# One projection of a hybrid trunk by one Strassen level, with sums that stay in PSUM and another place in the program

## The chip, the cores and the metric

The kernel runs on one core of one Trainium2 chip. The metric is the device time of one execution in microseconds (us). It is a float32 kernel whose large products run on TensorE (PE); VectorE (DVE), ScalarE (ACT), GpSimd (POOL) and the DMA queues of SyncE (SP) and POOL prepare operands and move data.

## The reference

One layer with D = 1024, 1024 tokens, batch 1, all in float32. What matters here:

```
h = RMSNorm_pre(x)
[s5_x | s5_gate | lru_x | lru_gate | merge_gate_s | merge_gate_l] = h @ W_in
S5 : y = Re(C s) + D u (diagonal SSM), GELU, GLU with w_glu (512 -> 2x512),
     times SiLU(s5_gate), then ps = y @ w_bs       (512 -> 1024)
LRU: conv, RG-LRU over 10 heads of 128 channels, times SiLU(lru_gate),
     then pl = yl @ w_bl                           (1280 -> 1024)
merged = sigmoid(merge_gate_s) * ps + sigmoid(merge_gate_l) * pl
mix = merged @ W_out                               (1024 -> 1024)
x = x + RMSNorm_post(mix); x = x + (p @ W_ple) * sigmoid(x @ W_ple_gate)
```

The change concerns `yl @ w_bl`: 8 output rows of 128 channels, each a sum over 10 heads, for 1024 tokens.

## The kernel before

**A product.** Every fp32 operand is split in two float32r parts, high and low. A 128x128 weight block times 512 tokens is then three matmuls (`three`: high x high, high x low, low x high) of 128x512, all into one PSUM bank of 128x512. A row of 8 weight blocks for all 1024 tokens is 48 matmuls; a w_bl row with its 10 heads is 60.

**Weights.** `W` streams them. A chunk of 512 KB (`wraw`, four buffers) comes over SP's queue; per group of four blocks ("quad"; `wq`, a ring of six) ACT copies the high part and DVE subtracts for the low part (L228, "a low"). For w_bs, w_out's plain part and w_ple_gate the low part is instead an ACT copy with a minus sign and an accumulating DMA from POOL's queue (L220). `W.ahead` prepares up to four quads ahead of the one in use, and `fetch` loads raw chunks further ahead; a quad in a plain product feeds 24 matmuls. Where one Strassen level is used (parts of W_in, and w_out), POOL adds up the weight sums (L188), and a quad then feeds 12 matmuls.

**Order.** PE, DVE, ACT and POOL issue in the order in which the program is written; the order on SP's queue is the scheduler's. Work that is written as a generator in `bg` (splits, merges) is advanced one step at each `tick`, between quads. PSUM has eight 128x512 banks: two belong to other products, and from the RG-LRU stage until after F the other six are three tiles of two banks (`wide`), which the products take in turn.

**The stages around the change.** `light(6)`, `light(7)` are two rows of W_in (silu gates of S5; `ps_L`, evicted by ACT L950 and DVE L952). Meanwhile head 9 of the RG-LRU ends on DVE with a scan over 1024 tokens (L1031) and a product (L1034). Then `bl((0, 1))`, `bl((2,))`: w_bl rows 0, 1, 2; the GLU products `eb0, ea0 ... eb3, ea3` (4 blocks each); w_bl rows 3 to 7; F: the eight rows of w_bs, each multiplied with its gate `gs` (`mg`, L1234), to which an accumulating DMA on POOL's queue (L1235) adds the row that `bl` left in DRAM (`ms_d`). The generator `merged` (L1176 to L1223) turns the finished `mg` rows into the operands of the Strassen w_out products, `mB`, `mT`. w_out begins with `oX` (operand `mB11` for four products, then `mB21` accumulated onto them), and goes on with `oY`, `oZ`, `oW`, `oV`.

The operands of w_bl, `yl` (high and low for each head), fill 10 pages of SBUF; head 9's raw row goes to DRAM (`yl_d`) and comes back. What is written of `bl` is short:

```
def bl(ds):
    for d in ds: load blg{d} from sgl_d
    products of 10 heads into ps (two rows share a pass where len(ds) > 1)
    V.tensor_tensor(gs[d], gs[d], t, ALU.mult)       # L1108, 128x1024
    nc.sync.dma_start(ms_d[d], gs[d])                # L1109
```

## Time and profile before

| | us |
|---|---|
| median of 3 runs (range) | 962.07 (961.91 to 962.28) |
| the profiled execution, its own time | 961.16 |
| span of its profile | 959.4 |
| PE busy | 945.0 of 959.4 (98%), 4308 matmuls |
| DVE, ACT, POOL busy | 598.8, 452.7, 161.0 |
| DMA moved | 128.19 MB |
| w_bl rows 0 to 2 | 582.0 to 622.8 |
| GLU | 622.8 to 667.15 |
| w_bl rows 3 to 7 | 667.15 to 735.0 |
| F | 735.0 to 780.8 |
| first oX products of w_out | 780.8 to 799.6 |

The profiled execution is 0.91 us below the median; 1.76 us of its time lie outside the span. Times in rows are microseconds from the start of the span. A line number is that of the kernel, or of the helper that issues the instruction: all matmuls of `three` carry L309, L310, L311. A matmul's duration (0.39 us for 128x512) overlaps the next one; the pitch from start to start is what it costs.

Of the kernel before, what the change touches and what calls it, by code (L numbers as in the profile page):

```python
# [36 lines left out]
def weight_plan():  # L37
# [11 lines left out]
    def col(name, m, ks):  # L49
        return [(name, k, m) for k in ks]  # L50
# [196 lines left out]
def tile_hybrid_trunk(  # L247
# [29 lines left out]
    yl_d = dram.tile([P, NT], F32, name="yl_d")  # L277
# [701 lines left out]
    yl_home = {m: i for m, i in enumerate((2, 3, 6, 7, 8, 9, 4, 5, 10, 11))}  # L979
    yl, yl_raw = {}, {}  # L980

    def yl_page(m):
        t = page(yl_home[m], f"yl{m}", F32).rearrange("p (s n) -> p s n", s=2)
        yl[m] = t.bitcast(F32R)
        return t

    def lru_head(m):
# [33 lines left out]
        def late():  # L1021
# [11 lines left out]
            t = l1.tile([P, NT], F32, tag=f"yr{m}", name=f"yr{m}") if m in (6, 7) else g  # L1033
            V.tensor_tensor(t, sq, g, ALU.mult)  # L1034
            yl_raw[m] = t
            if m == NL - 1:
                nc.sync.dma_start(yl_d, t)
            if m < 6:
                yl_page(m)
                S.activation(yl[m][:, 0], t, AF.Copy)  # L1040
                yield
                V.tensor_tensor(yl[m][:, 1], t, yl[m][:, 0].bitcast(F32), ALU.subtract)
# [51 lines left out]
    def ylr(k, h):  # L1094
        return yl[k][:, 0, HALF[h]], yl[k][:, 1, HALF[h]]

    def bl(ds):
        gs = {}
        for d in ds:
            gs[d] = h2.tile([P, NT], F32, tag=f"g{d % 2}", name=f"blg{d}")  # L1100
            nc.sync.dma_start(gs[d], sgl_d[d])
        if len(ds) > 1:
            ps = [wide(f"ps_bl{d}") for d in ds]
            two(NL, ylr, "bl", ps=[[t[:, HALF[h]] for h in range(2)] for t in ps])
        else:
            ps = [rows(ylr, f"bl{ds[0]}", nk=NL)]
        for t, d in zip(ps, ds):
            V.tensor_tensor(gs[d], gs[d], t, ALU.mult)  # L1108
            nc.sync.dma_start(ms_d[d], gs[d])  # L1109

    bg.append(gel_build())
    bl((0, 1))
    bl((2,))
    drain()

    ysf = [page(i, f"ysf{i}", F32).rearrange("p (k n) -> p k n", k=2) for i in range(2)]
# [6 lines left out]
    et = page(11, "et", F32).rearrange("p (i n) -> p i n", i=2)  # L1123
# [4 lines left out]
    def by_slot(t):  # L1128
        return t.rearrange("p (k j) -> p j k", j=8)

    ys = []
    for j in range(NS):
        t, y = et[:, j % 2], ysr(j)
        pb = rows(ger, f"eb{j}", nk=NS)
        S.activation(by_slot(t), pb.rearrange("p (j k) -> p j k", j=8), AF.Sigmoid)
        V.tensor_tensor(t, t, y, ALU.mult)
        pa = rows(ger, f"ea{j}", nk=NS)
        V.tensor_tensor(by_slot(y), by_slot(t), pa.rearrange("p (j k) -> p j k", j=8), ALU.mult)
# [12 lines left out]
    for d in range(3, ND):
        bl((d,))
    drain()

    mpg = ((7, 8, 12, 13), (14, 15, 16, 17))
# [15 lines left out]
    def op(name, i):  # L1171
        mop[name] = [quarter(page(i + s, f"m{name}{s}")) for s in range(2)]
# [310 lines left out]
```

### The profile page before, as it was taken

The page shows a single profiled execution, that of the slowest core. Times are in us where ns is not written, and L with a number is a line of the kernel's source. Part 1 is how long each engine was busy: PE and PEld are TensorE (multiplying, and loading weights), DVE is VectorE, ACT ScalarE, POOL GpSimd, SP SyncE. Part 2 cuts the span into 40 slices and gives each one's busy share as a digit, 9 for nine tenths or more (in the row PEclk, how much of TensorE's full clock was granted, in tenths as well). Part 3 has the DMA queues.
Part 4 walks back from the last instruction along what each step waited for, and adds up shares of the span by engine and source line. Part 5 has one row for each costly group of instructions (what it writes and reads, how often), then busy time and mean ns, then how long its engine had stood idle before and what let it go on. Part 6 is the DMA issues. An engine that isn't in the chain of part 4 may idle for free.

```text
span 959.4 us, 11815 instructions
## 1 busy us (share of the span) xinstructions
PE 945.0 (98%) x4308; PEld 775.4 (81%) x4308; DVE 598.8 (62%) x1019; ACT 452.7 (47%) x652; POOL 161.0 (17%) x178
## 2 busy tenths in 40 slices
PE   8999999999999999999999999999999999999998
PEld 6888888788888888888888888888888877887877
DVE  6976578788763337766666668245311469786842
ACT  6652243344343256676666665224112344558561
POOL 1318121222210000000000000000001244534431
PEclk9999999999999999999999999999999999999999
DMA  9754133323333201111111115742347995399995
GB/s 347 256 129 125 51 117 116 116 73 116 117 116 99 71 28 50 50 50 45 50 50 50 50 50 150 262 153 63 109 148 219 236 224 174 116 244 231 283 256 156
DMA packets 64282, 128.19 MB, mean 134 GB/s; under 512 B 18400, under 2 KB 29024, under 8 KB 64224
## 3 DMA queue, kind: packets, MB, share of 16 engines
q1 hardware_dynamic: 55584, 109.61, 35.2%
q0 software_dynamic: 8640, 17.83, 10.5%
q8 instruction: 34, 0.56, 0.2%
q14 instruction: 24, 0.20, 0.1%
HBM read 84.81 MB, written 27.79 MB: 117 GB/s over the span
## 4 chain that ended last, share of the span: by engine, by line
PE 77%; DVE 10%; issue 7%; DMA 2%; ACT 2%; POOL 1%; SPq 1%; POOLq 0%; DVEq 0%; ACTq 0%
PE ps_L L309 6%; PE ps_L L311 5%; PE ps_L L310 5%; PE ps_rx L309 4%; PE ps_rg L309 4%; PE ps_rg L311 4%; PE ps_rx L311 4%; PE ps_rg L310 4%; PE ps_rx L310 4%; PE ps_bl L310 4%; PE ps_bl L309 4%; PE ps_bl L311 4%; PE ps_pg L310 2%; PE ps_pg L311 2%; PE ps_pg L309 2%
## 5 line engine op out<-in xcount | busy, mean ns | idle before, releaser
L216 ACT ACTIVATE wq<-wraw 128x512 fp32r<-128x512 f32 (+1 forms) x189 | 112.3, 606 | 90.3 <-PE ps_bl L311 77.6
L220 POOL DMA_DIRECT2D wq<-wraw x52 | 47.8, 920 | 533.3 <-ACT wq L219 516.9
L309 PE MATMUL ps_L<-hB,wq 128*128 128x512 f32 x320 | 127.1, 397 | 0.0
L311 PE MATMUL ps_L<-hB,wq 128*128 128x512 f32 x320 | 124.7, 390 | 0.0
L310 PE MATMUL ps_L<-hB,wq 128*128 128x512 f32 x320 | 124.7, 390 | 0.0
L228 DVE TENSOR_TENSOR wq<-wraw,wq 128x512 fp32r<-128x512 f32 (+1 forms) x137 | 97.1, 728 | 4.7 <-ACT wq L216 4.7
L309 PEld LDWEIGHTS ps_L<-hB,wq 128*128 128x128 f32 x320 | 60.1, 188 | 13.4 <-issue 1.7
L311 PEld LDWEIGHTS ps_L<-hB,wq 128*128 128x128 f32 x320 | 60.1, 188 | 12.9
L310 PEld LDWEIGHTS ps_L<-hB,wq 128*128 128x128 f32 x320 | 60.1, 188 | 11.7
L997 DVE SCALAR_TENSOR_TENSOR c<-ps_rx,cp_t,c 128x1023 f32<-128x1023 f32 (+2 forms) x30 | 38.4, 1282 | 43.6 <-ACT c L995 42.9
L309 PE MATMUL ps_rx<-hB,wq 128*128 128x512 f32 x160 | 62.5, 391 | 0.0
L309 PE MATMUL ps_rg<-hB,wq 128*128 128x512 f32 x160 | 62.5, 391 | 0.0
L311 PE MATMUL ps_rx<-hB,wq 128*128 128x512 f32 x160 | 62.4, 390 | 0.0
L311 PE MATMUL ps_rg<-hB,wq 128*128 128x512 f32 x160 | 62.4, 390 | 0.0
L309 PE MATMUL ps_bl<-yl,wq 128*128 128x512 f32 x160 | 62.3, 389 | 0.0
L311 PE MATMUL ps_bl<-yl,wq 128*128 128x512 f32 x160 | 62.3, 389 | 0.0
L310 PE MATMUL ps_rx<-hB,wq 128*128 128x512 f32 x160 | 62.2, 389 | 0.0
L310 PE MATMUL ps_rg<-hB,wq 128*128 128x512 f32 x160 | 62.2, 389 | 0.0
L310 PE MATMUL ps_bl<-yl,wq 128*128 128x512 f32 x160 | 62.2, 389 | 0.0
L1108 DVE TENSOR_TENSOR blg<-blg,ps_bl 128x1024 f32<-128x1024 f32 x8 | 9.8, 1221 | 68.8 <-PE ps_bl L311 68.7
L950 ACT ACTIVATE sg<-ps_L 128x1024 f32<-128x1024 f32 x20 | 20.5, 1026 | 61.6 <-PE ps_L L311 45.1
L310 PE MATMUL ps_pg<-x1hl,wq 128*128 128x512 f32 x120 | 47.4, 395 | 0.8 <-DVE x1hl L1185 0.8
(347 smaller groups left out, 2184.7 us busy)
## 6 DMA issues: line engine op xcount, KB each, us to landing
wraw<-w_blocks SPq DMA_DIRECT2D x90, 512.0 KB, 4.1
wq<-wraw POOLq DMA_DIRECT2D x52, 256.0 KB, 6.6
xt<-x_t SPq DMA_DIRECT2D x8, 512.0 KB, 8.2
ple_d<-ple_sb SPq DMA_DIRECT2D x8, 512.0 KB, 4.9
sgl_d<-sg SPq DMA_DIRECT2D x8, 512.0 KB, 4.8
sgs_d<-sg SPq DMA_DIRECT2D x8, 512.0 KB, 4.6
blg<-sgl_d SPq DMA_DIRECT2D x8, 512.0 KB, 4.7
ms_d<-blg SPq DMA_DIRECT2D x8, 512.0 KB, 3.0
```

The lines of the kernel that those rows point to most:

```text
L216: nc.scalar.activation(hi, src, AF.Copy)
L220: nc.gpsimd.dma_start(lo.bitcast(F32), src, accum_op=ALU.add)
L228: self.nc.vector.tensor_tensor(lo, src, hi.bitcast(F32), ALU.subtract)
L309: T.matmul(ps, wh, xh, start=start, stop=False, skip_group_check=more)
L310: T.matmul(ps, wh, xl, start=False, stop=False, skip_group_check=more)
L311: T.matmul(ps, wl, xh, start=False, stop=stop, skip_group_check=more)
L950: S.activation(t, ps, AF.Sigmoid)
L997: V.scalar_tensor_tensor(c[:, d:], ps[:, :NT - d], w_[3 - d], c[:, d:], ALU.mult, ALU.add)
L1108: V.tensor_tensor(gs[d], gs[d], t, ALU.mult)
```

## The change

`w_bl` for heads 0 to 7 becomes a 2x2 Strassen product (Winograd's form, seven products): heads 0-3 and 4-7 against the two halves of the tokens, and pairs of output rows (2p, 2p+1). Heads 8 and 9 stay plain ("tails", `btail`). Per pair of rows the seven products are of four blocks for 512 tokens, 12 matmuls each.

- Ahead of GLU: products B11 for the four pairs (banks `bX0` to `bX3`), B21 accumulated onto the same banks, then the tails of the rows 0, 2, 4, 6 for the first half of the tokens, and their gates (`brow`, L1129). ACT keeps a copy of the B11 products (`bu`).
- GLU after it, each row in two banks evicted apart (`brows`).
- Then, for each of the four pairs: T2 into bank `bZ`, T1 into `bW`, a tail into `bV`, T3 onto `bZ`, a tail onto `bW`, B22 onto `bW`, a tail onto `bZ`, T4 onto `bZ`: 78 matmuls. The sums between products are made by DVE and ACT inside the banks.
- The operands (T1 to T4, B11, B21, B22: differences of token halves and heads, then the split) are new work on DVE and ACT: B21 after `light(7)`, T2 and T1 during GLU, T3, B22 and T4 between GLU and the first pair, and the split of the GLU's result `ys`, which stood in the GLU loop, during the first pairs.
- POOL makes the weight sums of the four pairs, 16 operations of 128x512.
- One pool of six single banks (`pp`) is opened after `light(7)` instead of after F, and F's rows are evicted by halves. `yl_d` and its round trip go.

Line numbers shift: L309 to L311 become L312 to L314, L228 becomes L232, L188 L192, L220 L224, L952 L958, L1034 L1054.

```diff
+    for ks in (lo, hi):                                   # order of the weights
+        for m in (0, 4):
+            plain(col("w_bl", m, ks) + col("w_bl", m + 2, ks))
+    plain([b for m in range(0, ND, 2) for b in col("w_bl", m, hi2)])
...
+        for part in ("O2", "S1", "P", "S3", "S4", "A22"):
...
+    lctx.close()
+    wide_ctx.close()
+    pp = ctx.enter_context(tc.tile_pool(name="pp", bufs=6, space=PSUM))
...
+    xs = [bank(f"bX{p}") for p in range(4)]
+    for p_ in range(4):
+        bprod(xs[p_], "B11", True)
+        S.activation(bu[:, p_, :], xs[p_], AF.Copy)
...
+    for p_ in range(4):
+        bprod(xs[p_], "B21", False)
...
+    def late_ops():
+        for name, i, j, q in (("T3", 12, 13, 12), ("B22", 14, 15, 22), ("T4", 0, 1, 21)):
+            bop(name, i, j)
+            for k in range(4):
+                bsplit(name, k, bq(q, k))
+            yield
+        yield
+        for j in range(NS):                                # split of ys
...
+    next(late_bl)
+    bg.append(late_bl)
+    for p_ in range(4):
...
+        z, w_, v = (bank(f"b{n}{p_}") for n in "ZWV")
+        bprod(z, "T2", True)
+        V.tensor_tensor(z, z, u, ALU.add)
+        S.activation(u, z, AF.Copy)
+        bprod(w_, "T1", True)
+        S.activation(gb[:, HT:], w_, AF.Copy)
+        V.tensor_tensor(w_, w_, u, ALU.add)
...
+        btail(v, wb[2:], 1, True)
...
+            three(z, b, (hi[:, k, :], lo[:, k, :]), False, k == 3, True)   # T3
...
+        btail(w_, wb[:2], 1, False)
...
+            three(w_, b, (hi[:, k, :], lo[:, k, :]), False, k == 3, True)  # B22
...
+        btail(z, wb[2:], 0, False)
+        bprod(z, "T4", False)
...
     for n, d in enumerate(F_ROWS):
         sgs_load()
-        ps = rows(ysr_, f"F{d}", nk=NS)
-        V.tensor_tensor(mgrow(d), gls[n], ps, ALU.mult)
+        for h, ps in enumerate(brows(ysr_, f"F{d}", NS)):
+            V.tensor_tensor(mgrow(d)[:, HALF[h]], gls[n][:, HALF[h]], ps, ALU.mult)
         G.dma_start(mgrow(d), ms_d[d], accum_op=ALU.add)
         bg.append(merged(d))
-    wide_ctx.close()
-    pp = ctx.enter_context(tc.tile_pool(name="pp", bufs=6, space=PSUM))
```

**Place 1, PE between `light(7)` and w_bl.** Before, the last matmuls of `light(7)` and the first of w_bl row 0 (`ps_bl0`, operand `yl0` and weights `wq102`):

```order
2445 L309 MATMUL ps_L7_4499<-hB220_440,wq101_4417 128x512
2446 L310 MATMUL ps_L7_4499<-hB221_441,wq101_4417 128x512
2447 L311 MATMUL ps_L7_4499<-hB220_440,wq101_4417 128x512
2448 L309 MATMUL ps_bl0_4630<-yl0_3076,wq102_4454 128x512 [waits PE_49,Activation_49]
2449 L310 MATMUL ps_bl0_4630<-yl0_3076,wq102_4454 128x512
2450 L311 MATMUL ps_bl0_4630<-yl0_3076,wq102_4454 128x512 [waits DVE_49]
2451 L309 MATMUL ps_bl0_4630<-yl0_3076,wq102_4454 128x512
```

Now, the same place, with the first product B11 (`bX0`):

```order
2445 L312 MATMUL ps_L7_4501<-hB220_439,wq101_4421 128x512
2446 L313 MATMUL ps_L7_4501<-hB221_440,wq101_4421 128x512
2447 L314 MATMUL ps_L7_4501<-hB220_439,wq101_4421 128x512
2448 L312 MATMUL bX0_4637<-bB112_2779,wq102_4458 128x512 [waits DVE_49]
2449 L313 MATMUL bX0_4637<-bB113_2780,wq102_4458 128x512
2450 L314 MATMUL bX0_4637<-bB112_2779,wq102_4458 128x512
```

The first matmul into `bX0` waits for DVE. The new pool gives `bX0` the bank that held the first half of `ps_L7`, whose last reader is DVE's L958; `ps_bl0` had another tile's banks. On DVE that reader stands at the end of head 9, as it did before (the scan and the two products ahead of it are the same, L1030, L1031, L1034, L952 there):

```order
726 L1050 TENSOR_TENSOR i9_4256<-i9_4256,ta9_4257 128x1024 [waits Activation_49]
727 L1051 SCALAR_TENSOR_TENSOR sq9_4258<-r9_4255,i9_4256 128x1024 [waits DVE_49]
728 L1054 TENSOR_TENSOR yr9_4569<-sq9_4258,g9_4254 128x1024 [waits DVE_49]
729 L958 TENSOR_TENSOR sg_7_4571<-sg_7_4571,ps_L7_4501 128x1024 [waits Activation_49]
730 L308 TENSOR_TENSOR bB211_4610<-yr2_3750,bB210_4609 128x512 [waits Activation_49] x2
731 L308 TENSOR_TENSOR bB211_4610<-yr3_4083,bB210_4609 128x512 [waits Activation_49] x2
```

What moved behind it: the splits of B21 and of heads 8 and 9 follow where the splits of heads 6 to 9 stood.

**Place 2, DVE from the end of GLU.** Before: the last GLU product, its split, head 9's row, the lows of the next quads, and the gate of w_bl row 3:

```order
763 L1138 TENSOR_TENSOR ysf1_4868<-et_4873,ps_ea3_5092 128x8x128 [waits DVE_49,PE_49]
764 L1141 TENSOR_TENSOR ys3_5125<-ysf1_4868,ys3_5125 128x1024 [waits Activation_49]
765 L228 TENSOR_TENSOR wq121_5093<-wraw69_4878,wq121_5093 128x512 [waits DMAHW4_49]
766 L1147 CAST yl9_5146<-yl9_5146 128x1024 [waits DMAHW3_49]
767 L1148 TENSOR_TENSOR yl9_5146<-yl9_5146 128x1024 [waits DVE_49]
768 L228 TENSOR_TENSOR wq122_5131<-wraw69_4878,wq122_5131 128x512 [waits Activation_49]
769 L228 TENSOR_TENSOR wq123_5162<-wraw70_5096,wq123_5162 128x256 [waits DMAHW2_49,Activation_49]
770 L1108 TENSOR_TENSOR blg3_5128<-blg3_5128,ps_bl3_5130 128x1024 [waits DMAHW6_49,PE_49]
```

Now, from the second half of the last GLU product to the add into `bW0` (x2 stands for two instructions; L308 is the low part of a split):

```order
785 L1207 TENSOR_TENSOR ysf1_4834<-et_4839,ps_ea31_5099 128x4x128 [waits PE_49]
786 L308 TENSOR_TENSOR bT313_5134<-yr0_3076,bT312_5133 128x512 [waits Activation_49] x2
787 L308 TENSOR_TENSOR bT313_5134<-yr1_3413,bT312_5133 128x512 [waits Activation_49] x2
788 L232 TENSOR_TENSOR wq123_5100<-wraw68_4848,wq123_5100 128x512 [waits DMAHW4_49,Pool_49]
789 L308 TENSOR_TENSOR bB2215_5166<-yr2_3750,bB2214_5165 128x512 [waits Activation_49] x2
790 L308 TENSOR_TENSOR bB2215_5166<-yr3_4083,bB2214_5165 128x512 [waits Activation_49] x2
791 L1237 TENSOR_TENSOR bZ0_5147<-bZ0_5147,bu_4636 128x512 [waits PE_49]
792 L232 TENSOR_TENSOR wq124_5150<-wS2_120_4962,wq124_5150 128x512 [waits Pool_49]
793 L232 TENSOR_TENSOR wq125_5177<-wraw68_4848,wq125_5177 128x512 [waits Activation_49]
794 L308 TENSOR_TENSOR bT41_5198<-yr2_3750,bT40_5197 128x512 [waits Activation_49] x2
795 L308 TENSOR_TENSOR bT41_5198<-yr3_4083,bT40_5197 128x512 [waits Activation_49] x2
796 L1241 TENSOR_TENSOR bW0_5148<-bW0_5148,bu_4636 128x512 [waits Activation_49]
```

Twelve splits of T3, B22 and T4 and three lows of quads now stand in one row around the two adds into banks, for which PE's products T3 (into `bZ0`) and the tail of `bW0` wait.

**Place 3, SP's queue before F.** Before, `gs0` and the first `gsp` are the gates of F's first two rows, `wraw80` is the last chunk of w_bs, `wraw81` and `wraw82` are the first two of w_out, `blg6`, `blg7` are w_bl's last rows:

```order
219 L1109 DMA ms_d_82<-blg5_5288 128x1024
220 L157 DMA wraw80_5403<-w_blocks 128x1024
221 L1101 DMA blg7_5448<-sgl_d_79 128x1024
222 L157 DMA wraw81_5455<-w_blocks 128x1024
223 L1109 DMA ms_d_82<-blg6_5370 128x1024
224 L1204 DMA gs0_5543<-sgs_d_80 128x1024
225 L157 DMA wraw82_5513<-w_blocks 128x1024
226 L1204 DMA gsp_5542<-sgs_d_80 128x1024
227 L1109 DMA ms_d_82<-blg7_5448 128x1024
228 L1204 DMA gsp_5542<-sgs_d_80 128x1024
229 L1204 DMA gs2_5546<-sgs_d_80 128x1024
230 L1204 DMA gs4_5580<-sgs_d_80 128x1024
```

Now (chunks count two higher: `wraw82` is the last of w_bs, `wraw83` the first of w_out; `ga2` to `gb3` are w_bl's last two pairs of rows, stored in halves; the first `gsp` is F's first gate):

```order
225 L1234 DMA gb3_5568<-sgl_d_79 128x512
226 L1130 DMA ms_d_82<-ga2_5437 128x512
227 L1233 DMA ga3_5567<-sgl_d_79 128x1024
228 L161 DMA wraw82_5615<-w_blocks 128x1024
229 L1130 DMA ms_d_82<-ga3_5567 128x512
230 L161 DMA wraw83_5650<-w_blocks 128x1024
231 L1130 DMA ms_d_82<-gb3_5568 128x512
232 L1315 DMA gsp_5709<-sgs_d_80 128x1024
233 L161 DMA wraw84_5680<-w_blocks 128x1024
234 L1130 DMA ms_d_82<-ga3_5567 128x512
235 L1315 DMA gsp_5709<-sgs_d_80 128x1024
236 L1315 DMA gs3_5714<-sgs_d_80 128x1024
```

Against the chunks the gates stand where they stood; between the last chunk of w_bs and F's first gate stood one load, one chunk and one store, and now a chunk and two half stores. What moved is the place of all of this against PE: a quad of the Strassen pairs feeds 12 matmuls where one of a plain row fed 24, so the four quads by which `W.ahead` and the chunks behind it run ahead of PE reach half as far before F's first product.

More of the change, by code (lines that the diff above doesn't have):

```diff
@@ L1092, in gel_build @@
             yield
[L1094 to L1109, printed above, removed]
@@ L1111, in tile_hybrid_trunk, with bprod, btail @@
-    bg.append(gel_build())
-    bl((0, 1))
-    bl((2,))
-    drain()
-    ysf = [page(i, f"ysf{i}", F32).rearrange("p (k n) -> p k n", k=2) for i in range(2)]
+    def bprod(ps, name, start):
+        W.ahead()
+        hi, lo = bops[name]
+        for k, wb in enumerate(W.next()):
+            three(ps, wb, (hi[:, k, :], lo[:, k, :]), start and k == 0, k == 3, not start)
+        tick()
+    def btail(ps, wb, h, start):
+        for k, w_ in zip((8, 9), wb):
+            three(ps, w_, (yl[k][:, 0, HALF[h]], yl[k][:, 1, HALF[h]]), start and k == 8, k == 9, not start)
@@ new lines, in brow @@
+    def brow(d, h, gt, ps):
+        V.tensor_tensor(gt, gt, ps, ALU.mult)
+        nc.sync.dma_start(ms_d[d][:, HALF[h]], gt)
+    bg.append(gel_build())
+    bu = quarter(page(18, "bu", F32))
+    xs = [bank(f"bX{p}") for p in range(4)]
+    gts = []
+    for p_ in range(4):
+        bprod(xs[p_], "B11", True)
+        S.activation(bu[:, p_, :], xs[p_], AF.Copy)
+        if p_ < 2:
+            gts.append(h2.tile([P, NT], F32, tag=f"g{p_}", name=f"bg{p_}"))
+            for i in range(2):
+                nc.sync.dma_start(gts[p_][:, HALF[i]], sgl_d[4 * p_ + 2 * i][:, HALF[0]])
@@ L1118, in ysr @@
+    ysf = [page(10 + i, f"ysf{i}", F32).rearrange("p (k n) -> p k n", k=2) for i in range(2)]
     def ysr(j):
@@ L1122, in tile_hybrid_trunk, with brows @@
         nc.sync.dma_start(ysr(j), sil_d[j])
-    et = page(11, "et", F32).rearrange("p (i n) -> p i n", i=2)
+    et = page(0, "et", F32).rearrange("p (i n) -> p i n", i=2)
+    btmp = quarter(page(1, "btmp", F32))
+    bg.append(t_ops())
     def ger(k, h):
         return geo[k][:, 0, HALF[h]], geo[k][:, 1, HALF[h]]
-    def by_slot(t):
-        return t.rearrange("p (k j) -> p j k", j=8)
-    ys = []
+    def brows(rhs, name, nk):
+        ps = [bank(f"ps_{name}{h}") for h in range(2)]
+        for k in range(nk):
+            if k % 4 == 0:
+                W.ahead()
+                wb = W.next()
+            for h in range(2):
+                three(ps[h], wb[k % 4], rhs(k, h), k == 0, k == nk - 1)
+            if k % 2:
+                tick()
+        return ps
@@ L1171, in op @@
     def op(name, i):
-        mop[name] = [quarter(page(i + s, f"m{name}{s}")) for s in range(2)]
+        mop[name] = [quarter(page(PG[i + s], f"m{name}{s}")) for s in range(2)]
     def lagged(lo, src, hi, eng=None, copy=False):
@@ L1413, in tile_hybrid_trunk @@
         squares[0].append(c)
-    plp, sbp = (quarter(page(i, n, F32)) for i, n in ((9, "plp"), (10, "sbp")))
+    plp, sbp = (quarter(page(PG[i], n, F32)) for i, n in ((9, "plp"), (10, "sbp")))
     drain()
```

159 lines of the change are left out of this document (105 added, 54 removed).

## Prediction

> **What bounds the kernel now.** I read the page's busy times first, then the chain that ended last, then a table of the stages around the change, then TensorE's waits.
>
> ```profile
> PE 945.0 (98%) x4308; PEld 775.4 (81%) x4308; DVE 598.8 (62%) x1019; ACT 452.7 (47%) x652; POOL 161.0 (17%) x178
> PE 77%; DVE 10%; issue 7%; DMA 2%; ACT 2%; POOL 1%; SPq 1%; POOLq 0%; DVEq 0%; ACTq 0%
> ```
>
> TensorE is busy for 98% of the span and carries 77% of the chain: it is the bound, and every matmul saved is worth its pitch, every new idle stretch of it its full length. The stages (columns: stretch, its length, busy time and count of each engine, granted TensorE clock, share of the DMA engines, GB/s):
>
> ```profile
> 582.00:622.80 40.80, 40.80 (x182) 33.78 (x181) 22.22 (x24) 12.65 (x17) 0.00 (x0) 1.00 0.61 213
> 622.80:667.15 44.35, 44.35 (x194) 36.17 (x193) 21.13 (x19) 15.10 (x14) 0.00 (x0) 1.00 0.33 110
> 667.15:735.00 67.85, 67.85 (x300) 56.15 (x300) 16.45 (x20) 12.70 (x22) 4.47 (x5) 1.00 0.46 137
> 735.00:780.80 45.80, 44.40 (x194) 35.92 (x192) 22.17 (x28) 14.89 (x26) 12.29 (x14) 1.00 1.00 238
> 780.80:799.60 18.80, 17.35 (x75) 14.05 (x76) 16.09 (x19) 10.69 (x21) 8.60 (x7) 1.00 0.87 210
> 799.60:845.00 45.40, 45.16 (x197) 36.69 (x196) 39.44 (x55) 21.22 (x40) 20.98 (x16) 1.00 0.50 150
> ```
>
> The first three rows are w_bl rows 0 to 2, GLU, and w_bl rows 3 to 7: TensorE without a gap, DVE a quarter to a half busy, DMA with room. F (fourth row) has the DMA engines full, and TensorE begins to wait at its end:
>
> ```profile
> engine line waited for: us in total, times, longest us
> PE oX L310 <- DVE mB L1185: 1.5, 1, 1.5
> PE oX L309 <- DVE mg L1234: 1.4, 1, 1.4
> ```
>
> These two are the longest waits of TensorE before the kernel's end; the change stands right ahead of them.
>
> **The matmuls removed.** w_bl has 480 matmuls, and 432 after: 7 products of 12 for each of four pairs of rows, 336, and 96 in the tails. 48 fewer, at 67.85/300 = 0.2262 us: -10.9 us, all on TensorE, which sets the end.
>
> **Their pitch.** The rows of w_out's Strassen products give (45.40 - 0.2 of a wait)/197 = 0.2294. If the 336 go at that, they cost 336 x 0.0032 = +1.1; if at w_bl's own, 0. I take +0.7, nearer to the row that has the same shape of product.
>
> **The bank of the first product.** Its first matmul waits for L958, the product on the gate of light row 7, which is L952 before:
>
> ```profile
> 580.89 1.23 DVE L1030 TENSOR_TENSOR i<-i,ta 128x1024 f32<-128x1024 f32 x1 [0.55 <-ACT ta L1028]
> 582.15 2.29 DVE L1031 TENSOR_TENSOR_SCAN sq<-r,i 128x1024 f32<-128x1024 f32 x1
> 584.48 1.23 DVE L1034 TENSOR_TENSOR g<-sq,g 128x1024 f32<-128x1024 f32 x1
> 585.62 1.21 DVE L952 TENSOR_TENSOR sg<-sg,ps_L 128x1024 f32<-128x1024 f32 x1
> 581.97 0.39 PE L309 MATMUL ps_bl<-yl,wq 128*128 128x512 f32 x1
> ```
>
> DVE comes to it at 585.62, behind head 9's scan and product, and has done at 586.83; TensorE is ready at 581.97. The operations on DVE ahead of it are the same in the same order, so nothing pulls it forward. From a DVE end to the matmul that waits for it pass some 0.15 us, as at the end of F:
>
> ```profile
> 779.40 1.22 DVE L1234 TENSOR_TENSOR mg<-gsp,ps_F 128x1024 f32<-128x1024 f32 x1 [0.72 <-PE ps_F L311]
> 780.77 0.48 PE L309 MATMUL oX<-mB,wq 128*128 128x512 f32 x1 [1.40 <-DVE mg L1234]
> ```
>
> So TensorE idles 586.98 - 581.97 = +5.0 (4.8 to 5.2). Behind the waiting matmul stands all of TensorE. The five microseconds let DVE's and ACT's preparation run ahead, so that I see no second stall in B11, B21 and the tails (DVE 22.2 of 40.8 busy there). GLU is evicted by halves, in the same DVE time.
>
> **The first pair after GLU.** Here DVE's row of splits is the limit. Prices:
>
> ```profile
> 667.19 2.27 DVE L1138 TENSOR_TENSOR ysf<-et,ps_ea 128x1024 f32<-128x1024 f32 x1 [1.66 <-PE ps_ea L311]
> 794.90 0.68 DVE L1185 TENSOR_TENSOR mB<-mg,mB 128x512 fp32r<-128x512 f32 x1
> 795.50 0.68 DVE L228 TENSOR_TENSOR wq<-wS,wq 128x512 fp32r<-128x512 f32 x1
> 784.53 0.64 ACT mT L1178
> 818.41 1.11 DVE L228 TENSOR_TENSOR wq<-wS,wq 128x512 fp32r<-128x512 f32 x1 [2.04 <-ACT wq L216]
> 820.04 1.41 DVE L228 TENSOR_TENSOR wq<-wraw,wq 128x512 fp32r<-128x512 f32 x1
> 788.07 1.63 POOL L188 TENSOR_TENSOR wS<-wraw 128x512 f32<-128x512 f32 x1
> ```
>
> A 128x512 operation costs DVE 0.60 us back to back, and now and then 1.1 to 1.4 (where POOL sums weights). From the end of GLU's last matmul: the last two half products (half of 2.27 each, the first begun earlier) end at 1.75; nine operations (T3 x4, a low, B22 x4) at 7.15; the add into `bZ0` at 7.75; ACT's copy of that bank, 0.64, at 8.4. TensorE wants `bZ0` for T3 after 30 matmuls, at 6.9: +1.6. Then two lows, four splits of T4 and the add into `bW0` end at 7.75 + 7 x 0.60 = 11.95 without the slow operations and 13.95 with three or so; TensorE wants `bW0` 12 matmuls after 8.5, at 11.25: +0.8 to +2.8. I take +2.2, since POOL's sums of the next pair (four of 1.63) fall into just this stretch. Sum +3.8 (2.4 to 4.4). In the later pairs DVE has at most four splits each, in 18 us: 0.
>
> **Other work, at no cost.** POOL's 16 sums, 26 us, lie in a stretch in which it is busy 4.5 of 112 us; their cover is POOL's idle time, and their price to DVE is in the term above. The copies and adds of ACT and DVE in the later pairs are some 10 operations in 18 us. The gates of w_bl come as halves over the same queue; `yl_d`'s two transfers go.
>
> **F and the start of w_out.** The wait that ends last is the chain of the rows of F:
>
> ```profile
> 725.00:735.00 10.00, 10.00 (x45) 8.28 (x45) 0.00 (x0) 2.31 (x4) 1.71 (x2) 1.00 0.90 249
> 735.00:745.00 10.00, 10.00 (x45) 8.15 (x44) 2.44 (x2) 2.31 (x4) 1.75 (x2) 1.00 0.92 263
> 775.00:785.00 10.00, 8.60 (x38) 6.75 (x38) 6.70 (x10) 4.45 (x8) 3.52 (x4) 1.00 0.93 189
> 785.00:795.00 10.00, 9.18 (x41) 7.28 (x39) 9.87 (x12) 5.00 (x10) 5.53 (x4) 1.00 0.95 251
> q0 software_dynamic: 2448, 6.55, 65.9%
> q1 hardware_dynamic: 1786, 6.48, 34.5%
> 714.94 1.02 POOL L220 DMA_DIRECT2D wq<-wraw  x1 [446.67 <-ACT wq L219]
> 733.96 0.85 POOL L220 DMA_DIRECT2D wq<-wraw  x1 [4.58 <-ACT wq L219]
> 778.37 5.34 DMA mg<-ms_d
> ```
>
> (The queue rows are of 735 to 790: packets, MB, share of the DMA engines.) The last row of the chain is a `mg` row's accumulating transfer, after which DVE makes `mB21`, at 794.90. POOL's five accumulating transfers for w_bs (first and last of them shown) are issued 20 to 1 us before F begins at 735.0. In the new order a quad lasts 12 matmuls, so by the lead of four quads I put the same five at 10 to 2 us before F, and the first chunk of w_out and the first gate behind them, about when F begins. A 512 KB transfer of SP's queue costs 0.345 x 55/6.48 x 0.52 = 1.5 us of all DMA engines, a 256 KB one of POOL's 0.659 x 55/6.55 x 0.26 = 1.45. Two of the first and one of the second, 4.5 us of work, come to lie behind F's start. The engines had some 2.0 us to spare there (shares 0.92, 0.93, 0.95 of 10 us each). So the chain would end 2.5 us later: +2.5. The bounds: -2.9, both stalls gone (1.4 + 1.5; the first, for the two-bank tiles, goes in any case, but the second then grows by as much unless the chain ends earlier), and +5, no spare time found.
>
> **Sum.** -10.9 + 0.7 + 5.0 + 3.8 + 2.5 = +1.1 on the profiled execution's 961.16, that is 962.3; it stands 0.9 under the median of 962.07, so the forecast is **963.2**. A change within 0.2% (1.9 us) can hardly be told from none.
>
> **Rivals.** *Faster: F has room.* If the transfers that come later find the DMA engines free in time (the stage before F has a share of 0.46, and the pairs end with TensorE held up 9 us, in which transfers go on), the last term is between -1.4 and 0: with 0 and the splits at 2.8, 962.07 - 10.9 + 0.7 + 5.0 + 2.8 = 959.7; with -1.4, 958.3. It is faster than can be mistaken once this term is under -0.5. Against it: a share of 1.00 over all of F. 0.31.
>
> *Slower: F pays in full.* With +5 the sum is 3.6, 965.7; it decides from +3.3 on. For it: a transfer that takes 5.3 us to land where its own work is 3, and a queue on which each waits for the ones before. 0.18.
>
> *Slower: the clock falls in the gap.* The trace shows the granted clock fall once, after the last matmul (end 954.78):
>
> ```profile
> 954.50 0.28 PE L311 MATMUL ps_pgz<-x1hl,wq 128*128 128x256 f32 x1
> 957.00:958.00 1.00, 0.00 (x0) 0.00 (x0) 0.00 (x0) 0.00 (x0) 0.00 (x0) 1.00 0.37 125
> 958.00:958.50 0.50, 0.00 (x0) 0.00 (x0) 0.00 (x0) 0.00 (x0) 0.00 (x0) 0.81 0.00 0
> 958.50:959.00 0.50, 0.00 (x0) 0.00 (x0) 0.00 (x0) 0.00 (x0) 0.00 (x0) 0.50 0.00 0
> ```
>
> From 1.00 to 0.50 at 958.3, 3.5 us after it. A gap of 4.85 us at `bX0` is longer than that, where none of before's in mid-kernel was over 1.5. How long the clock then stays low no row of mid-kernel shows; the program's first matmuls bound it:
>
> ```profile
> 1.06 4.64 PE L490 MATMUL warm<-ones 128*128 128x128 f32 x20 [1.06 <-DVE halfpi L284]
> 8.79 0.39 PE L309 MATMUL ps_ple<-p_hi,wq 128*128 128x512 f32 x1
> ```
>
> 20 small ones take 4.64 us, and from 8.79 the pitch is the usual one: at most 7.7 us at half pace, 3.9 us lost, and at least 0. At the middle, 2.0, the time is 965.2. One fall does not tell whether 3.5 us is short or long for it, and a short one would cost next to nothing: 0.18, on top of the forecast.
>
> The Trainium skill, TensorE: Matmul & The Clock Gate, Part 1: The HAM clock gate, speaks against this change here: after one idle window of about 3.4 us the clock is halved, and about 3.4 us of work bring it back; the window runs freely. The fall 3.5 us after the last matmul agrees. By its figures a gap of 4.85 us holds a whole window in about four cases of ten, and costs then, an estimate, 1.7 us: the sum would be +2.8 in those.
>
> *The change does not do what it says* would be 480 matmuls or a first product that does not wait; the order shows the count and the wait, so I give it nothing of its own. Without the wait the forecast would be 958.2, which is inside the range.
>
> **The numbers.** Forecast 0.33, F has room 0.31, F in full 0.18, clock 0.18. Faster by over 0.2% (below 960.1): four fifths of the first rival and a fifth of the forecast, whose terms are each uncertain by about 1, 0.32. The same: the rest of the first rival, three fifths of the forecast, and the lower fifth of the last two, 0.33. Slower: what is left, 0.35. The range goes from 957.5 (the last term at -1.4, the splits at 2.4, no cost in pitch) to 967.5 (+5, with the clock at about 2) and leaves out some 2 in 10.
>
> **What would show it.** A stall of TensorE of about 5.0 us at `bX` waited for on L958; two in the first pair, for `bZ` (1.6) and `bW` (about 2.2); none in the later pairs and in GLU; the four pairs together 312 matmuls in about 71 us and 3.8. In w_out, a wait at B21 on DVE's `mB` that is above 1.5, and none on F's `mg`; a DMA share that stays near 1.0 through all of F. The granted clock near 587 says whether it fell. I am wrong above all if F's chain does not move with the DMA work, or if splits in later pairs come late too.

## The result and the profile after

The changed kernel takes 971.7 us (median of 4, 970.88 to 972.43) against 962.17 before (the kernel of the table ahead of the prediction, with a fourth execution): ratio 1.0097, interval 1.008 to 1.0115. It is 1% slower, and above the range of the prediction (957.5 to 967.5). The profiled execution of the changed kernel took 971.6, its span is 969.8, 10.4 above that of before.

The page's busy row, and the same stages as before, cut at the first matmul of each, the first row where light(7) ends (w_bl's first part, GLU, the four pairs, F, oX, the start of the rest):

```profile
PE 942.1 (97%) x4260; PEld 770.3 (79%) x4260; DVE 639.9 (66%) x1102; ACT 476.4 (49%) x709; POOL 186.5 (19%) x194
581.77:615.64 33.87, 29.12 (x122) 23.78 (x121) 19.76 (x25) 17.94 (x27) 0.00 (x0) 0.95 0.54 173
615.64:659.86 44.22, 44.22 (x194) 36.04 (x193) 33.40 (x39) 20.03 (x30) 7.54 (x5) 1.00 0.40 135
659.86:738.14 78.28, 73.60 (x314) 59.59 (x312) 50.26 (x70) 30.63 (x56) 20.76 (x16) 0.98 0.47 137
738.14:781.66 43.52, 43.52 (x194) 36.05 (x192) 16.34 (x27) 11.55 (x20) 10.51 (x12) 1.00 1.01 262
781.66:809.69 28.03, 20.40 (x74) 14.88 (x73) 23.16 (x31) 15.68 (x30) 10.57 (x9) 0.88 0.84 200
809.69:855.00 45.31, 45.31 (x200) 37.23 (x199) 35.10 (x52) 19.47 (x35) 22.51 (x16) 1.00 0.49 145
```

The matmuls are 48 fewer and GLU is as long as it was. The two w_bl parts together take 112.2 us where they took 108.8. F and oX take 71.55 where they took 63.9 (735.03 to 798.94). Three rows have a granted clock under 1.00. What TensorE waited for, longest first:

```profile
engine line waited for: us in total, times, longest us
PE bX L312 <- DVE sg L958: 4.8, 1, 4.8
PE bW L312 <- DVE bW L1241: 3.1, 1, 3.1
PE oX L313 <- DVE mB L1296: 3.0, 2, 2.5
PE oX L312 <- ACT mB L1289: 2.8, 2, 1.9
PE oX L314 <- DMA wq<-wraw: 1.8, 2, 1.1
PE bZ L312 <- ACT bu L1238: 1.5, 1, 1.5
```

The first, second and last are the three stalls of the prediction. In oX there are 7.6 us where there were 2.9; in the later pairs and in GLU TensorE waits for nothing. Besides the matmuls and the waits there is the clock. These windows lie around the beginnings and ends of its falls (the last column but two is the granted clock):

```profile
586.00:588.00 2.00, 1.32 (x4) 1.08 (x5) 2.00 (x4) 1.99 (x3) 0.00 (x0) 0.79 0.28 111
588.00:589.00 1.00, 1.00 (x3) 0.73 (x3) 1.00 (x3) 0.00 (x0) 0.00 (x0) 0.50 0.92 314
590.00:591.00 1.00, 1.00 (x5) 0.82 (x4) 1.00 (x2) 0.00 (x0) 0.00 (x0) 0.71 0.43 93
675.00:676.00 1.00, 1.00 (x6) 0.83 (x5) 0.84 (x3) 1.00 (x3) 0.00 (x0) 0.96 0.00 0
679.00:680.00 1.00, 1.00 (x5) 0.77 (x5) 0.00 (x0) 0.00 (x0) 0.02 (x1) 0.84 0.01 4
802.00:803.00 1.00, 0.00 (x0) 0.00 (x0) 0.96 (x3) 0.00 (x0) 0.00 (x0) 0.60 0.54 94
809.00:810.00 1.00, 1.00 (x6) 0.82 (x5) 0.97 (x3) 1.00 (x4) 0.00 (x0) 0.98 0.73 156
```

If the clock is either 1.00 or 0.50, the first row puts the fall at 587.16, the third the return at 590.58; the others give 675.92 to 679.32 and 802.20 to 809.04. While it is low a matmul takes 0.63 us in place of 0.39, and the pitch is 0.43 in place of 0.23:

```profile
588.16 0.63 PE L313 MATMUL bX<-bB,wq 128*128 128x512 f32 x1
588.59 0.63 PE L314 MATMUL bX<-bB,wq 128*128 128x512 f32 x1
```

The first ten matmuls on `bX` take 3.98 us, where 2.3 would do: 1.7 lost. The 18 from 674.59 take 5.84 and not 4.10: 1.7. The 14 from 804.08 to oY take 5.61 and not 3.2: 2.4.

### The profile page after: what moved, and what is told of

Its sections match the earlier page's. It is cut to its first block, busy times and chain, and to the rows that moved or that the text cites. A ratio compares the mean times of both kernels' runs of the same rounds, so it can differ in the third digit from the quotient of the medians.

```text
span 969.8 us, 11935 instructions
## 1 busy us (share of the span) xinstructions
PE 942.1 (97%) x4260; PEld 770.3 (79%) x4260; DVE 639.9 (66%) x1102; ACT 476.4 (49%) x709; POOL 186.5 (19%) x194
## 4 chain that ended last, share of the span: by engine, by line
PE 72%; DVE 10%; issue 9%; DMA 3%; ACT 2%; POOL 2%; SPq 1%; POOLq 0%; DVEq 0%; ACTq 0%
PE ps_L L312 5%; PE ps_L L314 5%; PE ps_L L313 5%; PE ps_rx L312 4%; PE ps_rg L312 4%; PE ps_rg L314 4%; PE ps_rx L314 4%; PE ps_rx L313 4%; PE ps_rg L313 4%; PE ps_pg L314 2%; PE ps_pg L313 2%; PE ps_pg L312 2%; PE ps_u L313 1%; PE ps_u L314 1%; PE ps_u L312 1%
## 5 line engine op out<-in xcount | busy, mean ns | idle before, releaser
L312 PE MATMUL ps_L<-hB,wq 128*128 128x512 f32 x320 | 127.1, 397 | 0.0
L220 ACT ACTIVATE wq<-wraw 128x512 fp32r<-128x512 f32 (+1 forms) x188 | 112.8, 613 | 28.3 <-issue 11.8
L314 PE MATMUL ps_L<-hB,wq 128*128 128x512 f32 x320 | 124.7, 390 | 0.0
L232 DVE TENSOR_TENSOR wq<-wraw,wq 128x512 fp32r<-128x512 f32 (+1 forms) x136 | 99.4, 745 | 14.4 <-ACT wq L220 12.4
L192 POOL TENSOR_TENSOR wS<-wraw 128x512 f32<-128x512 f32 x8 | 14.2, 1779 | 383.1 <-DMA wraw<-w_blocks 368.2
L312 PEld LDWEIGHTS ps_L<-hB,wq 128*128 128x128 f32 x320 | 60.1, 188 | 13.4 <-issue 1.7
L314 PEld LDWEIGHTS ps_L<-hB,wq 128*128 128x128 f32 x320 | 60.1, 188 | 12.9
L224 POOL DMA_DIRECT2D wq<-wraw x52 | 47.5, 913 | 93.1 <-ACT wq L223 58.3
L312 PE MATMUL ps_rx<-hB,wq 128*128 128x512 f32 x160 | 62.5, 391 | 0.0
L312 PE MATMUL ps_rg<-hB,wq 128*128 128x512 f32 x160 | 62.5, 391 | 0.0
L314 PE MATMUL ps_rx<-hB,wq 128*128 128x512 f32 x160 | 62.4, 390 | 0.0
L314 PE MATMUL ps_rg<-hB,wq 128*128 128x512 f32 x160 | 62.4, 390 | 0.0
L956 ACT ACTIVATE sg<-ps_L 128x1024 f32<-128x1024 f32 x20 | 20.5, 1024 | 61.6 <-PE ps_L L314 45.1
L314 PE MATMUL ps_pg<-x1hl,wq 128*128 128x512 f32 x120 | 47.5, 395 | 1.5 <-DMA wq<-wraw 1.5
L313 PE MATMUL ps_pg<-x1hl,wq 128*128 128x512 f32 x120 | 47.4, 395 | 0.0
L312 PE MATMUL ps_pg<-x1hl,wq 128*128 128x512 f32 x120 | 47.2, 393 | 0.0
```

The source lines that it names most:

```text
L192: G.tensor_tensor(s[name], s[a], s[b], op)
L220: nc.scalar.activation(hi, src, AF.Copy)
L224: nc.gpsimd.dma_start(lo.bitcast(F32), src, accum_op=ALU.add)
L232: self.nc.vector.tensor_tensor(lo, src, hi.bitcast(F32), ALU.subtract)
L312: T.matmul(ps, wh, xh, start=start, stop=False, skip_group_check=more)
L313: T.matmul(ps, wh, xl, start=False, stop=False, skip_group_check=more)
```

## The experiments

The first seven start from the changed kernel (971.7), the others, where nothing else is said, from the run with three edits together. Edits are shown shortened.

**Another bank for the first product.** A memset of one column of one more bank, ahead of the four sums, so that `bX0` gets a bank that head 9's gate product held:

```diff
+    V.memset(bank("other")[:, :1], 0.0)
     xs = [bank(f"bX{p}") for p in range(4)]
```

> The changed kernel with one more bank taken ahead of the four bX banks (a memset of one column on DVE), so that bX0 gets a bank that the gate product of head 9 held and that has long been free, instead of a bank of light row 7. Theory A (the bank, as the prediction's text on the change has it): the first matmul no longer waits for L958; the stall of 4.8 us and the slow matmuls behind it (1.7) go, some 965 us. Theory B (it is the opening of the new pool that waits for the last reader of all tiles of the old one, whatever bank is taken): the stall stays at 4.7 to 4.9 us, and the time at 971.7 within 0.8.

One execution, 973.1, which is 0.6 above the time that theory B allowed; the wait is unchanged:

```profile
PE bX L312 <- DVE sg L958: 4.8, 1, 4.8
```

The wait is as theory B has it and does not belong to the bank. The section on the change and the prediction named the bank of `ps_L7` as its reason; that is wrong. In these two runs the new pool's first tile waits for the last reader of the old pool's tiles, whichever bank it gets; the next two runs, which keep the old pool, start without this wait. The time differs by the clock: here it was low for 6.83 us from 586.29 on, and did not fall in the first pair at all, with the same wait of 3.1.

**The old pool for the first part.** The new pool opened ahead of GLU, the four sums as halves of two tiles of the old one:

```diff
-    wide_ctx.close(); pp = ...        # now behind the first part's drain()
+    xw = [wide("bXa"), wide("bXb")]
+    xs = [xw[p % 2][:, HALF[p // 2]] for p in range(4)]
```

> The changed kernel with the four bX sums in two tiles of the old two-bank pool, and the new pool opened only after the first w_bl part, ahead of GLU. Theory B: the 4.8 us stall at the first product is gone, and the granted clock stays at full speed near 587; against that, the third product waits for ACT's copy of the first (about 1.3 us, because two sums share a tile), the fourth for its weights' low part (about 1), and GLU's first product for the last gate product (about 1): 971.7 - 4.8 - 1.7 + 3.3 = 968.5, range 965.5 to 970. Rival (DVE and ACT are behind by the same time anyway, so the stall only moves to the operands of B21 and of GLU): 971 to 972.

Measured 974.55, ratio to before 1.0128 (1.0113 to 1.0143): slower than the changed kernel, outside both expectations. TensorE starts at once, and stops for as long at the third product:

```profile
PE bXa L312 <- ACT bu L1137: 4.7, 1, 4.7
591.97 0.60 ACT L1137 ACTIVATE bu<-bXa 128x512 f32<-128x512 f32 x1 [3.39 <-DVE yl L308]
```

ACT's copy of the first sum cannot start before DVE has split heads 8 and 9 (the copy's page lies where their raw rows were), and the third product, in the other half of the same tile, waits for that copy. My expectation had put the copy at its place on ACT and overlooked the page.

**A tile for each sum.** Three in first halves of old-pool tiles, the fourth in a bank beside the pools:

```diff
+    xs = [wide(f"bX{p}")[:, HALF[0]] for p in range(3)]
+    xs.append(px.tile([P, HT], F32, tag="px", name="bX3"))
```

> As the run with the old pool kept for the first part (the new one opened ahead of GLU), but with each of the four sums in a tile of its own: three in the first halves of the old pool's tiles, the third of them in that of light row 7, the fourth in a bank beside the pools. Theory (the 4.7 us at the third product of that run was my sharing of a tile between two sums, whose copy on ACT waits for pages of heads 8 and 9): the first two products start without a wait at 582, the third by 587 to 588, the fourth waits about 1 us for its weights' low part, GLU's first product 1.1 for the pool: 971.7 - 4.8 - 1.7 + 2.2 = 967.4, range 966 to 969. Rival (operands of B21 are as late as before, so that all of it comes back there): 971 to 972.5.

Measured 968.01, ratio 1.006 (1.0043 to 1.0077), as expected: the start at 582.7, two waits of 1.4 (the fourth product's weights) and 1.1 (GLU) left.

```profile
PE bX L314 <- DVE wq L232: 1.4, 1, 1.4
PE ps_eb L312 <- ACT geo L1110: 1.1, 1, 1.1
```

**Both adds ahead of the splits.**

```diff
-        bprod(z, "T2", True)          # ends with tick()
+        bprod(z, "T2", True, False)
         V.tensor_tensor(z, z, u, ALU.add)
         S.activation(u, z, AF.Copy)
+        tick()                         # and the same for W
```

> The changed kernel with the two adds into banks of each pair (Z+u, W+u) written ahead of the background step that follows them, so that on DVE they stand ahead of the splits of B22 and of T4. Theory (the two stalls of the first pair are DVE's order and nothing else): the stalls for bZ (1.5 in the list of waits) and bW (3.1) go or fall under 0.5 each, and with them the slow clock from 676 to 680 (1.7 us): 971.7 - 1.6 - 3.2 - 1.7 = 965.2, range 964 to 967. Rival (DVE and ACT have more work in the first pair than its 18 us hold, so that the wait moves to the splits of B22 and T4): stalls at B22 or T4 of 2 us or more in place of these, 968 to 971.

Measured 966.57, ratio 1.0046 (1.0029 to 1.0063): 5.1 us off, inside the range. The wait at bZ is gone, that at bW is 1.2 (under 0.5 was expected), and the clock is 1.00 from 660 to 690. So the two stalls are DVE's order; the rest at bW is the four splits of B22 and two lows that still stood ahead of the second add.

**The clock alone.** 39 matmuls into a bank that nothing reads, in the gaps at `bX0`, `bZ` and `bW`:

```diff
+    def spin(n, wt, xt_):
+        for _ in range(n):
+            T.matmul(busy, wt, xt_, start=True, stop=True)
```

> The changed kernel with 39 more matmuls of 128x512 into a bank that nothing reads, put where TensorE waits: 20 ahead of the first product (4.5 us of the 4.8 us gap), 7 or less in the gap at bZ (6) and 13 in that at bW. No wait is removed. Theory (the slow matmuls at 587 to 590 and 676 to 680 come from the granted clock, which falls in a gap of 3.5 us or a little more): the clock stays at 1.00 from 560 to 700, no matmul there takes over 0.5 us, and the time falls by 1.7 + 1.7 to 968.3, range 967.3 to 969.3. Rival (the slow pace is a cost of starting on new operands or banks after a wait): the same slow matmuls, 971 to 972.5.

Measured 968.14, ratio 1.006 (1.0045 to 1.0076): 3.6 us off with 39 matmuls more and every wait left in place. The windows have the full clock:

```profile
580.00:600.00 20.00, 19.79 (x88) 16.07 (x87) 14.93 (x18) 13.37 (x21) 0.00 (x0) 1.00 0.37 108
660.00:680.00 20.00, 19.63 (x85) 15.44 (x85) 18.09 (x27) 8.23 (x16) 4.61 (x3) 1.00 0.17 45
```

That settles for these two places that the slow matmuls are the clock's, and that an idle TensorE causes its fall. In oX, where nothing was filled, it still falls, in this execution twice.

**The gates of F.**

```diff
-    gsp = page(PG[11], ...)           # even gates; odd ones in g0, g1
+    PG[6] and PG[11] change places; gates 0, 1, 4, 5 in gsp, the others in g0, g1
+        if p_ == 3:                   # ahead of the last pair's T3
+            sgs_load()
+            sgs_load()
```

> The changed kernel with the gates of F's first two rows loaded into a page that is free 17 us before F (the two halves of what was the page of the last mg rows, with which it changes places) and written ahead in the last pair, instead of into a page that the tail of the last pair still reads and a buffer whose row has yet to be stored. Theory G (the chain of F is late because DVE waits 5.5 and 8.3 us for these two loads, which stand on SP's queue behind waits): DVE's first two mg products start 2 to 3 and 4 to 5 us earlier against F's start, the last mB21 split moves from 65.9 to 61 to 62 us after F's start, the clock no longer falls at 802, TensorE's waits in oX fall from 7.6 to about 3: 971.7 - 4.5 - 2.0 = 965.2, range 963.5 to 967. Rival D (it is late because the DMA engines have 4.5 us more work to do behind F's start, whatever the order): the mg products come earlier, but the accumulating transfers take longer to land by as much; the last split stays at 64 or later and the time at 969.5 to 972.

Measured 969.13, ratio 1.007 (1.0055 to 1.0085): 2.6 off, between the two ranges. In the changed kernel DVE waited twice for a load in F's first rows:

```profile
744.52 1.28 DVE L1345 TENSOR_TENSOR mg<-gsp,ps_F 128x512 f32<-128x512 f32 x2 [5.50 <-DMA gsp<-sgs_d]
754.13 1.28 DVE L1345 TENSOR_TENSOR mg<-gs,ps_F 128x512 f32<-128x512 f32 x2 [8.33 <-DMA gs<-sgs_d]
```

and in this run it waits for the products only (F starts here at 739.36, there at 738.14):

```profile
744.32 1.37 DVE L1350 TENSOR_TENSOR mg<-gsp,ps_F 128x512 f32<-128x512 f32 x2 [4.07 <-PE ps_F L314]
749.76 1.37 DVE L1350 TENSOR_TENSOR mg<-gsp,ps_F 128x512 f32<-128x512 f32 x2 [4.08 <-PE ps_F L314]
```

The matmul that waits for the last mB21 split stands 65.94 us after F's start in the changed kernel (804.08), 60.61 before, and 61.58 here (800.94). Theory G holds for 4.4 of the 5.3 us: the two products start 1.4 and 5.6 us earlier against F's start, and the waits in oX fall from 7.6 to 4.4, where about 3 was expected. The time falls by less, since F and oX end only 4.1 earlier: the clock still falls, the two waits at the end of oX are still 1.9 and 2.5, and this execution was later by 1.2 ahead of w_bl and by as much behind oX, in stages that the edit does not touch.

**Three edits together.** A tile for each sum; in each pair both adds ahead of any step, with one step less; the gates.

> Three edits on the changed kernel: the old pool kept for the first part, with a tile for each sum; in each pair both adds into banks ahead of any background step (one step less per pair, so that the two lows for the next quads are all that stands between them); F's first two gates in the page that is free early. Theory (the three losses are independent of each other): -4.3 for the pool, -6.6 for the first pair (1.5 and 3.1 in the list of waits, and the slow clock), -2.6 for the gates: 971.7 - 13.5 = 958.2, range 956 to 960.5; that is 4 us under the kernel before. Rival (what is taken from one wait turns up at the next): 963 or more.

Measured 957.82, ratio 0.9955 (0.9942 to 0.9968), as expected. So nothing of the three losses came back at another wait. It is not a test of exact sums: alone, the three runs gave 3.7, 5.1 and 2.6, 11.4 in all, and together 13.9, with an edit of the pairs that goes further than the one tried alone.

**And matmuls in oX's gap.** 18 into a bank that nothing reads, ahead of the fourth block of the first product on `mB21`.

> The three edits together, and 18 matmuls more into a bank that nothing reads, ahead of the fourth block of the first oX product on mB21, where TensorE waits some 4 us in all. Theory (what is left at the start of w_out is the chain's end, which TensorE must wait for, and a clock that falls in that wait and costs 2 us more): the clock stays at 1.00 there, and the time is 1.5 to 2.0 us under the run of the three edits, 956.4 where that gives 958.2. Rival (the extra matmuls only take the place of the wait, or push the product back): the same time as that run within 0.7.

Measured 956.25, ratio 0.9939 (0.9925 to 0.9952): the lowest median of all, 1.6 under the run without them. The clock in 785 to 795 us, first of the three edits, then with the matmuls:

```profile
785.00:795.00 10.00, 6.48 (x18) 4.97 (x19) 9.93 (x15) 7.59 (x16) 3.10 (x2) 0.66 0.63 187
```
```profile
785.00:795.00 10.00, 9.40 (x42) 7.44 (x41) 9.96 (x11) 5.86 (x12) 5.37 (x4) 1.00 0.67 181
```

The clock stays up, as forecast; that this is worth 1.6 us is not shown. Two of the six executions took 957.8, as long as the middle one without the matmuls, and the profiled one is among them. In it F and oX take 66.59 us to the start of oY, against 66.87 without: the matmul that waits for the last mB21 split stands 63.3 us after F's start, not 61.6. Why the split came later there is open.

**Less DMA work around F.** Low parts of w_bs by DVE, on the three edits and on the kernel before:

```diff
-    BY_DMA = ("w_bs", "w_out", "w_ple_gate")
+    BY_DMA = ("w_out", "w_ple_gate")
```

> The three edits together, with the low parts of w_bs made by DVE's subtraction as for w_bl, in place of an ACT copy and an accumulating transfer of 256 KB each on POOL's queue: eight such transfers (8 x 1.45 = 11.6 us of all DMA engines) leave the stretch around F, and eight DVE operations of 0.6 us come in. Theory D (what is left of the late chain at the start of w_out is DMA work): the mg rows' transfers land 1.5 to 3 us sooner, the last mB21 split comes 2 to 4 us earlier than 61.6 us after F's start, the clock no longer falls there, and the time is 3 to 5 us under the 957.8 of the three edits. Rival (the end of that chain is DVE's own row of merges, some 12 us behind the last row's transfer): the split at 61 or later, the time 957 to 959.

> The kernel before the change with the same one edit (w_bs's low parts by DVE). It tells whether the DMA work around F is a price of the change or was there before it. Theory D: the last mB21 split, 60.6 us after F's start, comes 1.5 us or more earlier, both stalls at the start of w_out shrink from 2.9 to 1.4 or less (the first, on F's last product, stays), 960.5. Rival: no change, 961.7 to 962.7.

On the three edits 957.23, ratio 0.9941 (0.9923 to 0.9959), which overlaps that of the edits alone; the split still holds TensorE until 61.4 us after F's start, with the same waits of 2.5 and 1.8: the rival. On the kernel before 962.9, ratio 0.9995 (0.9982 to 1.0008): no change in the median. With the three edits the amount of DMA work thus does not set the end of the chain. For the kernel before it stays open: in the profiled execution the second stall is gone, as theory D had it, but that one (959.4) is the fastest of ten, and the others do not bear out a gain.

**The order of F's last merges.** On the three edits: the last row's mB21 and mT2 ahead of the row before's mT3; in the first run the mT1 operands later too, in the second not.

```diff
         op_split("T2", k, t)
+        flush()
         yield
+        if d == 6:
+            yield
+            yield
```

> The three edits together, and F's last merges in another order on DVE: the mB21 and mT2 operands of the last two rows first, their mT3 operands and the first mT1 operands behind them. No work is removed. Theory (the end of the chain at the start of w_out is DVE's row of merges behind the last two rows' transfers): the last mB21 split comes at 51 to 55 us after F's start instead of 61.6, TensorE's two waits there (1.9 and 2.5) go, the clock stays at 1.00, and at most 3 us come back as waits for mT3 in oZ: 957.8 - 4.4 - 2.0 + 0 to 3 = 951.5 to 954.5. Rival (the rows' transfers set the end): the split at 60 or later, 957 to 959.

> As the last run, but with the mT1 operands where the changed kernel has them; only the mT3 operand of the last row but one is put behind the last row's mB21 and mT2. Theory (in the last run the wait moved to oW because I had put the mT1 operands too far back): no wait at oW; the last mB21 split near 59 us after F's start, 1 to 1.5 us of wait left at oX and up to 2 at oZ, the clock at 1.00: 957.8 - 3.0 = 954.8, range 953.5 to 956.5. Rival (DVE's work behind the last transfers is simply as long as TensorE's lead, so that any order gives a wait of 4 to 5 us and a slower clock somewhere in oX to oW): 957 to 959.

The first: 962.34, ratio 0.9989 (0.9981 to 0.9998), outside both expectations. The second: 957.09, ratio 0.9938 (0.9921 to 0.9954), in the rival's range and not to be told from the three edits. In the first the wait at oX shrank to 1.2, and two others came in its place:

```profile
PE oW L312 <- DVE mT L1304: 4.2, 1, 4.2
PE oZ L314 <- DVE wq L232: 2.1, 1, 2.1
```

In the second 1.9 and 1.2 stay at oX, and the clock falls. Behind the last transfers DVE has some 16 us of merges and lows in a row (from 777.24 on in the run of the three edits); in these two orders TensorE meets their end somewhere. Whether another order, or another engine for a part of them, would clear it was not tried. Nor was another place for POOL's weight sums. In the changed kernel they fall into just this row, and three of DVE's operations beside them take 5.7 us, where three others take about 0.6 each:

```profile
796.45 2.28 DVE L1334 TENSOR_TENSOR mg<-mg,mtmp 128x512 f32<-128x512 f32 x1
796.57 1.61 POOL L192 TENSOR_TENSOR wS<-wraw 128x512 f32<-128x512 f32 x1
798.25 1.62 POOL L192 TENSOR_TENSOR wS<-wS,wraw 128x512 f32<-128x512 f32 x1
798.65 3.43 DVE L1296 TENSOR_TENSOR mT<-mg,mT 128x512 fp32r<-128x512 f32 x2
```

That is some 3.9 us, by estimate, of a chain for whose end TensorE waits 4.4; the kernel before has the same slow operations (2.30 and 3.48).

## Why the prediction was wrong

Terms of the sum, as forecast and as the profiles show them:

| | forecast | measured |
|---|---|---|
| 48 matmuls | -10.9 | -10.9 (4260 in the page) |
| pitch | +0.7 | +0.9 (222 matmuls from 687.30 to 738.14: 0.2290) |
| first product | +5.0 | +4.9 |
| first pair | +3.8 | +5.0 (1.7 and 3.3) |
| F and the start of w_out, without the clock | +2.5 | +5.2 |
| the clock | 0 in the sum | +5.8 (1.7, 1.7, 2.4) |

They add up to +10.9 against +10.4 in the span; the stages that are not in the table are 0.5 shorter. (The prediction's 0.2262 came from a window that opens 0.16 us behind the first matmul; from 666.99 to 735.03 it is 0.2268, which leaves -10.9 as it is.)

- *The bank of the first product*: right in place and size, wrong in its reason (the pool's opening, not the bank). The prediction saw no second stall behind it because the five microseconds let the preparation run ahead; that is borne out, for 2.5 us of waits come back once the stall is gone.
- *The first pair*: right in place; the second stall passed its upper bound of 2.8. Two rows show why: one low took 1.48 us and the four splits of T4 3.58, where 0.6 each was the price, with POOL summing weights from 668.57 to 671.57, and ACT held up a low by 0.59.

```profile
668.93 1.48 DVE L232 TENSOR_TENSOR wq<-wraw,wq 128x512 fp32r<-128x512 f32 x1 [0.59 <-ACT wq L220]
670.34 3.58 DVE L308 TENSOR_TENSOR bT<-yr,bT 128x512 fp32r<-128x512 f32 x4
```

- *F and the start of w_out*: the wrong mechanism. I priced DMA work that falls behind F's start; the runs show two loads that come late because of where they go: F's first gate into a page that the last pair's tail still read, the second into a buffer whose row was stored behind a weight chunk's wait on SP's queue. SP's queue shows it: the first gate leaves at 736.84, when the tail is done (its last matmul starts at 735.17), the next chunk holds the queue until 741.68, and the store of `ga` and the loads `gs`, the second gate among them, come behind it:

```profile
736.84 0.38 SPq L1315 DMA_DIRECT2D gsp<-sgs_d  x1
741.68 0.33 SPq L161 DMA_DIRECT2D wraw<-w_blocks  x1
742.07 0.45 SPq L1130 DMA_DIRECT2D ms_d<-ga  x1
743.09 3.77 SPq L1315 DMA_DIRECT2D gs<-sgs_d  x2
```

Place 3 of the order has the first gate (232), the chunk and the store (233, 234), and ends just ahead of the second gate; I had compared places among the chunks and not asked what each waits for. That term was 2.7 too small. The prediction gave as its sign of being wrong that F's chain does not move with the DMA work; with less of it on the three edits, the split came at 61.4 us where it had come at 61.6.
- *The clock* is the step that failed most. It was a rival with 0.18 for one fall on top of the forecast, and with nothing in the sum, though all the terms of the sum that I forecast as idle time of TensorE are just the gaps that make it fall. In the profiled execution it fell three times, at the first product, in the first pair and in oX; the filling matmuls took 3.6 us off for the first two. The Trainium skill (TensorE: Matmul & The Clock Gate, Part 1: The HAM clock gate) has a low clock after an idle window of about 3.4 us, a freely running one. These runs agree with the length and the free run (next section but one), but the windows that brought the clock down here were 14, 39 and 27% busy, not idle. Its price of 1.7 us for the first gap, worked out in the prediction as an estimate, is what was measured in the profiled execution. The chance there, four cases of ten, was too low: in all five runs with a wait of 4.7 or 4.8 us in w_bl's first part the clock fell. The range (957.5 to 967.5; its terms give 957.2 to 967.7) had room for one fall of 2.0 beside F in full, not for three.
- *F has room* (959.7) is refuted; *F in full* came nearest in size (+5), by another cause.

## What to carry to other kernels

Here a bound TensorE paid for a gap twice: count the gap, and then ask if it leaves a stretch of some 3.4 us mostly idle, which cost another 1.7 us or more in this kernel. Before trusting a saving in matmuls, follow each newly waiting instruction to the exact release (a pool's opening, a page's last reader, a store further up the queue), for loads as for matmuls; here edits at three such places (the pool, the adds of the pairs, F's gates) turned 1% slower into 0.5% faster. Where a queue of small operations sits ahead of an add that TensorE waits for, write the add first.

## What the runs showed of the hardware

The falls and returns of the clock lie on one grid. From 587.16 to 590.58 and 675.92 to 679.32 are 3.42 and 3.40 us, from 802.20 to 809.04 twice 3.42; from the first fall to the second are 88.76 us, 26 x 3.414, and from there to the third 126.28, 37 x 3.413. In every other run with more than one fall they lie on such a grid too, which stands elsewhere in each execution. The fall comes at the end of such a stretch, and can so hit work that has begun again: at 675.92 TensorE had been back at work since 674.59. The three stretches that ended in a fall were not idle, but 14, 39 and 27% busy (the first time is TensorE's busy time):

```profile
583.76:587.17 3.41, 0.49 (x2) 1.00 0.00 0
672.51:675.92 3.41, 1.33 (x6) 1.00 0.21 87
798.79:802.20 3.41, 0.94 (x3) 1.00 0.93 270
```

All fourteen profiles, each cut by its own grid, give a bound (from 15 to 940 us, stretches at the full clock): each of the 20 stretches that were less than 45% busy ended in a fall; of the eight between 45 and 53% four did; none above did. So whether a wait costs the clock depends on where the grid lies. The wait of 3.1 us at `bW` brought it down in four of five runs; in the run with another bank its stretch was 46% busy, and it did not fall. The stalls of 1.4 to 1.5 us in the kernel before left no stretch under 59%.
